# Two rwkv layers: where the convolution's products, the norm of x, adaLN and conv_in(x) stand in the order of the work

## The chip, the cores and the metric

The kernel runs on one core of one Trainium2 chip. The metric is the device time of one execution in microseconds (us), lower is better. The kernel before takes 2877.57 us (median of three runs, 2877.03 to 2883.01).

## What is computed

Two blocks of two layers each, on 256 rows of 1024 features, in float32. The change touches the first block. Each of its layers takes x and a second sequence, ctx, through the same weights (cut to what matters):

```python
mod_x = silu(c) @ ada_w[l] + ada_b[l]          # adaLN: six rows of 1024 each for x, and the same for ctx
ux = modulate(rmsnorm(x, g1), sh1, sc1) @ w_in[l]
uc = modulate(rmsnorm(ctx, g1), csh1, csc1) @ w_in[l]
prep_c = rwkv_prep(uc[..., CONV_IN:], ...)
yc, s_f, s_b = rwkv_scans(prep_c, zero, zero, emit=not last)
prep_x = rwkv_prep(ux[..., CONV_IN:], ...)
yx, _, _ = rwkv_scans(prep_x, s_f, s_b, emit=True)
mix_x = concat([conformer_conv(ux[..., :CONV_IN], ...), rwkv_out(yx, prep_x, ...)])
x = x + gt1 * (mix_x @ w_out[l])
x = x + gt2 * swiglu(modulate(rmsnorm(x, g2), sh2, sc2), wg, wu, wd)
# layer 0 only: the same for ctx, with conformer_conv(uc[..., :CONV_IN]) and rwkv_out(yc, prep_c)

def conformer_conv(u, w, b, g, h):
    val, gate = split(u, 2)
    z = dwconv(val * sigmoid(gate), w) + b     # 31 taps along the sequence, 512 channels
    return silu(group_norm(z, 8, g, h))
```

`rwkv_scans` is a recurrence over 256 positions in both directions with a 64 x 64 state for each of eight heads. `rwkv_out` is a group norm of its result, a bonus term and a gate. The second block (feed-forward, a mixer, feed-forward, with layer norms) is not touched.

## The kernel before

All weights come from device memory in pieces of 128 x 1024 floats (512 KB) through a pool of four buffers (`raw`, L356; `NRAW` is 4), issued on SyncE's queue (SP) in the order in which the pieces are used. Most of them are split by ScalarE and VectorE into a rounded part `wh` (L349) and a rest `wl` (L350), and three products replace one (`mm3`, L343). The weights of adaLN and the diagonal matrices of the convolution are used whole, straight from `raw`.

**The recurrence.** `rwkv` (L767) works in chunks of 64 positions. First come the input products (`w_in`, L642), then per pair of heads the decays and the small triangular matrices, then `inverse`, a loop of 31 steps on VectorE (two instructions each), then `reads` and `values`, and then the chain: two groups of heads, four steps each, where a state is multiplied on TensorE and updated on VectorE (L1095 to L1134). At the end (L930 and after) stand a group norm of the result (`group_norm`, L747), the bonus (L938, L939) and the gate (L940); their products take the tile `gl` and the weights `gup`.

Layer 0 runs this on ctx in the mode "wide", then on x in the mode "half". Layer 1 runs it on ctx ("all") and on x in the mode "wide". The change concerns the two wide passes: ctx of layer 0, x of layer 1. Beside a wide pass runs other work, in lane "b":

- `conv_in` (weights `wc`): the 1024 columns of the convolution's input, eight pieces, result z = value times sigmoid(gate) (L679), four tiles. In a wide pass z lies in the buffer of x0.
- `conv_pe` (weights `cd`): the 31 taps as products with diagonal matrices, 16 pieces, result in the buffer of x1, then the convolution's group norm (L753, L755, L761, L762).
- `ada_steps` (weights `ada`): 32 pieces for four of the six rows of adaLN. Four pieces make a group: 16 products of 512 columns, a copy to the tile T2b by ScalarE (L505) and eight small products of T2b, then an addition (L511).

In the kernel before these three form one row of steps, from which `fill` takes six (`FILL`) after each of the eight chain steps; what is left over comes when its results are needed. In layer 0 the norm of x (`norm_x`, its transposes are L446) is emitted at the place "post", behind the chain, and conv_in of x behind everything; the convolution of x then runs on GpSimd (POOL), tap by tap (`conv`, L732 to L737), in the background of the next half pass.

**What sets the order.** The program emits instructions; each gets a priority by its place of emission. The framework's scheduler goes through an estimated time line and gives each engine, among the instructions that it takes to be ready, the one with the foremost priority. `later(n)` moves what is emitted inside it back by n places (`LATER`, 1500). On the chip each engine, and each DMA queue, then works strictly in that order.

After the wide pass of layer 0, ctx is loaded again into x0 and x1 (L1524); after that of layer 1 the copy `keep` is (L1505). These loads stand in SP's queue among the weights and wait until z and the convolution's result have been read.

## Time and profile before

| | |
|---|---|
| median of three runs | 2877.57 us |
| the profiled execution | 2879.11 us |
| its span, first to last instruction | 2877.3 us |
| mean granted clock of TensorE | 0.959 of full speed |
| TensorE busy (products) | 2731.5 us, 95% |
| weight loads of TensorE (beside products) | 2376.7 us, 83% |
| VectorE busy | 1635.5 us, 57% |
| ScalarE busy | 1311.4 us, 46% |
| GpSimd busy | 450.9 us, 16% |
| read from device memory | 441.90 MB, 154 GB/s over the span |

Busy times are shares of the whole span, over stages with different limits; they don't say what limits a stage. For that, the timeline and the waits of the stage are read. PE is TensorE, PEld its weight loads, DVE is VectorE, ACT ScalarE, POOL GpSimd, SP SyncE. A tile's name stands without its buffer number. Products on TensorE are pipelined, so the ends given for them overlap a little.

### The profile page before, as it was taken

The numbers are of one execution on the slowest core, as the hardware profiler recorded it, in microseconds if no ns is written. First come the engines' busy times: TensorE is split into PE (matmuls) and PEld (weight loads), VectorE is DVE, ScalarE is ACT, GpSimd is POOL, SyncE is SP. The second block draws the span as 40 slices with busy tenths as digits, with TensorE's granted clock in tenths as the row PEclk, the third lists the DMA queues.
The fourth block names the chain that finished last, engine by engine and source line by source line (L and its number), as shares of the span: only waits on it lengthen the run. The fifth ranks groups of instructions, "written<-read, shape, count | busy, mean of one in ns | idle before, by whom it ended". The sixth has DMA issues, their size and how long they took to land.

```text
span 2877.3 us, 54424 instructions
## 1 busy us (share of the span) xinstructions
PE 2731.5 (95%) x22894; PEld 2376.7 (83%) x22894; DVE 1635.5 (57%) x2579; ACT 1311.4 (46%) x1990; POOL 450.9 (16%) x425
## 2 busy tenths in 40 slices
PE   7899897999989998999889999999999999999998
PEld 4886586888768897887489889889899899889897
DVE  3833367855668455842355565665655655665655
ACT  5522355443456346521244454554544544644543
POOL 0200299980121001200000000010000000100000
PEclk8989998999999999979999999999999999999999
DMA  6324642433512344213745465443465555525553
GB/s 242 113 75 144 229 171 84 170 137 133 183 67 98 128 170 169 99 60 123 251 141 189 169 206 188 166 155 110 168 200 188 179 189 185 185 81 169 198 187 120
DMA packets 123377, 447.53 MB, mean 156 GB/s; under 512 B 13686, under 2 KB 14198, under 8 KB 123132
## 3 DMA queue, kind: packets, MB, share of 16 engines
q1 hardware_dynamic: 123132, 444.06, 44.6%
q8 instruction: 179, 2.93, 0.4%
q14 instruction: 66, 0.54, 0.1%
HBM read 441.90 MB, written 2.10 MB: 154 GB/s over the span
## 4 chain that ended last, share of the span: by engine, by line
PE 83%; DVE 8%; ACT 4%; DMA 3%; issue 1%; POOL 1%; SPq 0%; ACTq 0%; DVEq 0%; POOLq 0%
PE pb L341 38%; PE acc L341 25%; PE ps L341 19%; DVE wl L350 2%; DMA raw<-in_ada 2%; DVE x L629 1%; ACT wh L349 1%; PE acc L446 0%; DVE S L965 0%; ACT L392 0%; DMA raw<-in_wr 0%; DVE S L852 0%; DVE T L963 0%; DVE T2b L628 0%; POOL tap L736 0%
## 5 line engine op out<-in xcount | busy, mean ns | idle before, releaser
L350 DVE TENSOR_TENSOR wl<-raw,wh 128x1024 fp32r<-128x1024 f32 (+1 forms) x654 | 812.0, 1245 | 629.3 <-ACT wh L349 398.3
L349 ACT CAST wh<-raw 128x1024 fp32r<-128x1024 f32 (+1 forms) x654 | 682.1, 1046 | 899.6 <-PE pb L341 344.8
L341 PE MATMUL pb<-xf,wh 128*128 128x256 f32 (+1 forms) x2560 | 485.7, 288 | 13.3 <-DVE S L639 4.0
L341 PE MATMUL pb<-S,wh 128*128 128x256 f32 x2560 | 487.5, 288 | 3.4 <-DVE S L639 1.4
L341 PEld LDWEIGHTS pb<-xf,wh 128*128 128x128 f32 (+1 forms) x2560 | 408.2, 193 | 29.1 <-DVE T1b L596 7.3
L341 PEld LDWEIGHTS pb<-S,wh 128*128 128x128 f32 x2560 | 407.8, 192 | 17.3 <-issue 8.1
L341 PE MATMUL ps<-S,wh 128*128 128x256 f32 x2048 | 391.3, 288 | 1.1 <-ACT S L468 0.9
L341 PE MATMUL pb<-xf,wl 128*128 128x256 f32 (+1 forms) x1280 | 369.5, 289 | 2.1 <-DVE wl L350 2.0
L341 PE MATMUL pb<-S,wl 128*128 128x256 f32 x1280 | 366.9, 287 | 1.6 <-DVE wl L350 1.6
L341 PEld LDWEIGHTS ps<-S,wh 128*128 128x128 f32 x2048 | 327.5, 192 | 10.8 <-issue 4.2
L341 PE MATMUL ps<-S,wl 128*128 128x256 f32 x1024 | 293.8, 287 | 1.2 <-DVE wl L350 1.2
L373 POOL TENSOR_TENSOR wl<-raw,wh 128x1024 fp32r<-128x1024 f32 x22 | 53.7, 2453 | 1367.4 <-ACT wh L372 941.1
L341 PEld LDWEIGHTS pb<-xf,wl 128*128 128x128 f32 (+1 forms) x1280 | 247.1, 193 | 8.5 <-DVE wl L350 3.5
L341 PEld LDWEIGHTS pb<-S,wl 128*128 128x128 f32 x1280 | 245.5, 192 | 5.4 <-issue 2.6
L341 PE MATMUL acc<-wh,T 128*128 128x512 f32 x704 | 206.3, 393 | 0.0
L341 PEld LDWEIGHTS ps<-S,wl 128*128 128x128 f32 x1024 | 196.8, 192 | 3.5 <-DVE wl L350 1.6
L341 PE MATMUL acc<-wh,T1b 128*128 128x512 f32 x528 | 157.6, 396 | 3.5 <-ACT T1b L349 3.5
L341 PEld LDWEIGHTS acc<-wh,T 128*128 128x128 f32 x704 | 127.0, 189 | 23.7
L736 POOL TENSOR_SCALAR tap<-z,cols 128x255 f32<-128x255 f32 (+14 forms) x120 | 143.3, 1203 | 0.0
L737 POOL TENSOR_TENSOR z<-z,tap 128x255 f32<-128x255 f32 (+14 forms) x120 | 117.6, 980 | 4.1
L341 PE MATMUL pb<-x,raw 128*128 128x254 f32 (+15 forms) x496 | 115.7, 389 | 0.0
L341 PE MATMUL acc<-wl,T 128*128 128x512 f32 x352 | 113.1, 395 | 0.0
(444 smaller groups left out, 3828.5 us busy)
## 6 DMA issues: line engine op xcount, KB each, us to landing
raw<-in_fu SPq DMA_DIRECT2D x132, 512.0 KB, 3.2
raw<-in_ada SPq DMA_DIRECT2D x96, 512.0 KB, 4.4
raw<-in_pu SPq DMA_DIRECT2D x88, 512.0 KB, 3.2
raw<-in_qu SPq DMA_DIRECT2D x88, 512.0 KB, 4.3
raw<-in_fd SPq DMA_DIRECT2D x66, 512.0 KB, 3.2
raw<-in_wr SPq DMA_DIRECT2D x51, 512.0 KB, 3.4
raw<-in_pd SPq DMA_DIRECT2D x44, 512.0 KB, 3.3
raw<-in_qd SPq DMA_DIRECT2D x44, 512.0 KB, 4.2
```

The source lines that it names most:

```text
L341: return self.nc.tensor.matmul(out, lhsT, rhs, start=start, stop=stop, **kw)
L349: self.nc.scalar.copy(hi, src)
L350: self.nc.vector.tensor_sub(lo, src, hi.bitcast(F32))
L373: self.nc.gpsimd.tensor_sub(lo, r, hi.bitcast(F32))
L629: nc.vector.tensor_add(x[b][:, s], x[b][:, s], t)
L736: nc.gpsimd.tensor_scalar(t[:, d], z[:, f, s], w(j), None, ALU.mult)
L737: nc.gpsimd.tensor_add(zc[f][:, d], zc[f][:, d], t[:, d])
```

## The change

`rwkv` gets an argument `beside`, which it calls inside `later(LATER)` right behind the rest of the input products, and so ahead of the inverse. `wide` passes a function there that emits conv_in and conv_pe of the layer whole. The chain's filler is now a row of steps given by the caller: in layer 0 the norm of x, then adaLN's 32 pieces, then conv_in of x; in layer 1 adaLN alone. What is left over is emitted when `rwkv` is done. `norm_x` at "post" and the loop over conv_in(x) behind the pass are gone, and so are the constants `QB` and `QE`.

```diff
--- before.py
+++ after.py
@@ -39,7 +39,7 @@
 
 TAPS = sorted(range(31), key=lambda j: abs(j - 15))
 
-QB, QE, QC, EVERY = (2, 3, 4, 5), (2, 3, 4, 5), (1,), 2
+QC, EVERY = (1,), 2
 
 FILL = 6
 LATER = 1500
@@ -764,7 +764,8 @@
                 put(f, ys[f])
 
 
-    def rwkv(self, l, win, s0, emit, mode, fill=lambda n=1: None):
+    def rwkv(self, l, win, s0, emit, mode, fill=lambda n=1: None, beside=lambda: None):
+
 
 
 
@@ -825,6 +826,7 @@
                 self.on("b")
             for _ in win:
                 pass
+            beside()
             self.on("r")
         AR, GR, KB = [], [], []
         Ld, Lo = slab([P, 2, 4, 4, 32]), self.S([P, 2, 4, 4, 32])
@@ -1423,26 +1425,23 @@
         fl = lambda t: t.rearrange("p (a b) -> p a b", a=4)
         z = lambda: self.t(self.pool, [P, 4, T], "z", bufs=2)
 
-        def wide(l, x, s0, ada, perm, before=None):
-
-            def filler():
-
-                steps = itertools.chain(self.conv_in(l, x, fl(self.x[0])), self.conv_pe(l, fl(self.x[0]), fl(self.x[1])),
-                                        self.ada_steps(l, ada))
-
-                def fill(n=1):
-                    lane = self.lane
-                    self.on("b")
-                    for _ in range(n):
-                        next(steps, None)
-                    self.on(lane)
-
-                return fill
+        def wide(l, x, s0, steps, perm):
+
+            def conv():
+                drain(self.conv_in(l, x, fl(self.x[0])))
+                drain(self.conv_pe(l, fl(self.x[0]), fl(self.x[1])))
+
+            def fill(n=1):
+                lane = self.lane
+                self.on("b")
+                for _ in range(n):
+                    next(steps, None)
+                self.on(lane)
 
             self.pstags = alone
-            for at in self.rwkv(l, self.w_in(l, x, RW), s0, True, "wide", filler()):
-                if at == "post" and before is not None:
-                    before()
+            drain(self.rwkv(l, self.w_in(l, x, RW), s0, True, "wide", fill, conv))
+            self.on("b")
+            drain(steps)
             self.pstags = beside
             self.on("b")
             return self.mixed_in(fl(self.x[1]), self.y, perm)
@@ -1453,22 +1452,19 @@
         cf = self.norm1(0, cf, 1, False, self.xf)
         early = []
 
-        def norm_x():
+        def then_x():
+
             zt = lambda: self.t(self.pool, [P, D], "z", bufs=2)
-            self.on("b")
             early.append(self.norm1(0, self.load("x", [zt(), zt()]), 0, False, self.Sr, keep=True))
-            self.on("r")
-
-        cm = wide(0, cf, None, QB, False, norm_x)
+            yield
+            yield from self.ada_steps(0, (2, 3, 4, 5))
+            early.append(z())
+            yield from self.conv_in(0, *early)
+
+        cm = wide(0, cf, None, then_x(), False)
         states = self.states
         self.on("b")
-        (xf,) = early
-        zx = z()
-        mods = self.ada_steps(0, [q for q in (2, 3, 4, 5) if q not in QB])
-        for _ in self.conv_in(0, xf, zx):
-            next(mods, None)
-            next(mods, None)
-        drain(mods)
+        xf, zx = early
         win = self.w_in(0, xf, RW)
         ux = next(win)
         drain(win)
@@ -1500,7 +1496,7 @@
         for b in range(2):
             nc.sync.dma_start(self.keep[b], self.x[b])
         xf = self.norm1(1, self.x, 0, True, self.xf, acc=True)
-        xm = wide(1, xf, states, QE, True)
+        xm = wide(1, xf, states, self.ada_steps(1, (2, 3, 4, 5)), True)
         for b in range(2):
             nc.sync.dma_start(self.x[b], self.keep[b])
         f = self.out(1, self.x, 0, xm)
```

Where the scheduler puts the moved work is shown at three places.

TensorE, layer 0, at the end of ctx's chain, before (`raw,csil` are adaLN's products, `const,T2b` those that close a group; `acc<-xf,S` and `ps<-S,st` belong to the chain, `S,const` to the group norm of its result):

```order
L341 MATMUL acc_458_2881<-T_456_2878,S_1786 64x64
L341 MATMUL ps_2904<-S_1098,st_2701 64x64 x2
L341 MATMUL pb_2525<-const,T2b_2523 128x2 x4
L341 MATMUL pb_2531<-raw_2532,csil 32x512 x2
L341 MATMUL ps_3008<-S_1867,const 128x256
L341 MATMUL acc_492_3014<-S_1867,const 128x256
L341 MATMUL pb_2531<-raw_2536,csil 32x512 x2
L341 MATMUL acc_459_2892<-xf_1606,S_1434 64x64
L341 MATMUL acc_459_2892<-xf_1607,S_1434 64x64
```

Now, from the last transposes of x on; the chain's last product stands 24 rows ahead of this piece:

```order
L446 MATMUL pb_2398<-const,z_2365 128x128
L446 MATMUL pb_2398<-const,z_2366 128x128
L341 MATMUL pb_2447<-raw_2448,csil 32x512 x2
L341 MATMUL pb_2447<-raw_2452,csil 32x512 x2
L341 MATMUL pb_2447<-raw_2456,csil 32x512 x2
L341 MATMUL pb_2447<-raw_2460,csil 32x512 x2
L341 MATMUL acc_532_3292<-T_531_3289,const 128x256
L341 MATMUL acc_535_3304<-T_531_3289,const 128x256
L341 MATMUL ps_3316<-T_531_3289,const 128x256
L341 MATMUL pb_2466<-const,T2b_2464 128x2 x4
L341 MATMUL acc_536_3308<-rks_1648,const 128x256
```

The first groups of adaLN stood among the chain's last products; now all of them stand behind the chain, the first products of the norm and the sixteen transposes of x, and the gate's products (`gl`, `rks`) follow the first group.

TensorE, layer 1, before:

```order
L341 MATMUL ps_14642<-S_12794,st_14439 64x64 x2
L341 MATMUL pb_14263<-const,T2b_14261 128x2 x4
L341 MATMUL pb_14269<-raw_14270,csil 32x512 x2
L341 MATMUL acc_2453_14664<-S_13563,const 128x256
L341 MATMUL acc_2455_14670<-S_13563,const 128x256
L341 MATMUL pb_14269<-raw_14274,csil 32x512 x2
L341 MATMUL acc_2448_14630<-xf_13302,S_13130 64x64
L341 MATMUL acc_2448_14630<-xf_13303,S_13130 64x64
L341 MATMUL acc_2448_14630<-xf_13302,S_13130 64x64
```

Now, from the last products of the gate on; the chain's last product stands 24 rows ahead:

```order
L341 MATMUL acc_2469_14719<-gl_11997,S_14661 128x256 x2
L341 MATMUL ps_14731<-rks_13344,const 128x256
L341 MATMUL ps_14731<-gl_11997,S_14661 128x256 x2
L341 MATMUL pb_13034<-T1b_13023,const 128x256
L341 MATMUL pb_13038<-T1b_13023,const 128x256
L341 MATMUL acc_2471_14727<-T_2461_14688,const 128x256
L341 MATMUL pb_14082<-raw_14083,csil 32x512 x2
L341 MATMUL pb_14082<-raw_14087,csil 32x512 x2
L341 MATMUL pb_14082<-raw_14091,csil 32x512 x2
L341 MATMUL pb_14082<-raw_14095,csil 32x512 x2
L341 MATMUL pb_14101<-const,T2b_14099 128x2 x4
```

Before, adaLN's groups were mixed with the chain's last step, the norm and the gate. Now the norm and the gate (`pb<-T1b,const` is the convolution's norm, `acc<-T,const` and `gl` are the recurrence's) are done when the first group begins.

SyncE's queue of transfers, layer 0, before (x_67 is x0, x_68 is x1):

```order
L356 DMA raw_2519<-in_ada 128x1024
L1524 DMA x_67<-in_ctx 128x1024
L356 DMA raw_2532<-in_ada 128x1024
L356 DMA raw_2536<-in_ada 128x1024
L356 DMA raw_2594<-in_ada 128x1024
L356 DMA raw_2598<-in_ada 128x1024
L1524 DMA x_68<-in_ctx 128x1024
L356 DMA raw_2611<-in_ada 128x1024
```

Now:

```order
L356 DMA raw_2460<-in_ada 128x1024
L1520 DMA x_67<-in_ctx 128x1024
L1520 DMA x_68<-in_ctx 128x1024
L931 DMA S_3262<-in_gup 128x1024
L356 DMA raw_2473<-in_ada 128x1024
```

Both loads of ctx and the gate's weights now stand behind the first four pieces of adaLN, ahead of the other 28.

## Rows read from the trace of the kernel before

**Rows 1.** The page: busy times, and the chain that ended last by engine.
```profile
PE 2731.5 (95%) x22894; PEld 2376.7 (83%) x22894; DVE 1635.5 (57%) x2579; ACT 1311.4 (46%) x1990; POOL 450.9 (16%) x425
...
PE 83%; DVE 8%; ACT 4%; DMA 3%; issue 1%; POOL 1%; SPq 0%; ACTq 0%; DVEq 0%; POOLq 0%
```

**Rows 2.** Windows, layer 0: us, busy PE, PEld, DVE, ACT, POOL; PEclk, DMA share, GB/s.
```profile
157.00:189.00 32.00, 32.00 (x452) 27.27 (x450) 10.37 (x18) 10.49 (x16) 1.90 (x2) 0.80 0.15 51
...
290.00:328.00 38.00, 28.70 (x140) 10.69 (x140) 6.32 (x16) 9.88 (x20) 0.00 (x0) 0.89 0.88 311
```

**Rows 3.** Timeline of SP's queue, layer 0: start, us, line, transfer, count.
```profile
275.12 0.33 SPq L1524 DMA_DIRECT2D x<-in_ctx  x1
275.54 38.32 SPq L356 DMA_DIRECT2D raw<-in_ada  x24
```

**Rows 4.** Groups of PE, 269 to 279.7 us (layer 0): busy, mean ns, idle before.
```profile
L341 PE MATMUL pb<-raw,csil 128*32 128x512 f32 x30 | 6.9, 775 | 0.2 <-DMA raw<-in_ada 0.2
...
L341 PE MATMUL pb<-const,T2b 128*128 128x2 f32 x8 | 1.1, 254 | 0.0
```

**Rows 5.** Timeline of PE, layer 0: start, us, operation, count, idle before.
```profile
269.00 3.13 PE L341 MATMUL pb<-raw,csil 128*32 128x512 f32 x16
...
279.12 0.57 PE L341 MATMUL ps<-S,xf 128*64 128x64 f32 x12
...
294.14 1.05 PE L341 MATMUL pb<-const,T2b 128*128 128x2 f32 x8 [0.74 <-ACT T2b L505]
...
321.33 1.05 PE L341 MATMUL pb<-const,T2b 128*128 128x2 f32 x8 [0.74 <-ACT T2b L505]
322.25 0.69 PE L446 MATMUL pb<-const,z 128*128 128x128 f32 x4
...
327.80 0.80 PE L341 MATMUL pb<-S,wh 128*128 128x256 f32 x2 [0.56 <-ACT T1b L462]
```

**Rows 6.** Groups of PE, 327.8 to 363 us (layer 0).
```profile
L341 PE MATMUL acc<-gl,S 128*128 128x256 f32 (+1 forms) x12 | 3.7, 411 | 0.0
L341 PE MATMUL acc<-T,const 8*128 8x256 f32 x4 | 1.4, 426 | 0.0
L341 PE MATMUL ps<-gl,S 128*128 128x256 f32 (+1 forms) x4 | 1.3, 428 | 0.0
```

**Rows 7.** Timeline of POOL, layer 0.
```profile
343.35 0.94 POOL L732 TENSOR_SCALAR z<-z,cols 128x256 f32<-128x256 f32 x1 [5.75 <-DVE z L679]
...
346.59 0.73 POOL L939 TENSOR_TENSOR S<-S,T 128x256 f32<-128x256 f32 x1
347.26 0.30 POOL L890 MEMSET rks<- 128x256 f32 x1
```

**Rows 8.** Windows, 460 to 470 us, columns as in the second group.
```profile
460.00:470.00 10.00, 3.69 (x63) 3.11 (x66) 10.00 (x13) 3.66 (x8) 10.00 (x9) 0.80 0.00 0
```

**Rows 9.** Waits of PE, 430 to 485 us: total, times, longest.
```profile
PE ps L341 <- DVE S L851: 10.1, 3, 5.5
```

**Rows 10.** Windows, layer 1, columns as in the second group.
```profile
1255.00:1290.00 35.00, 33.95 (x426) 28.99 (x426) 10.38 (x23) 11.52 (x19) 0.95 (x1) 0.57 0.10 31
```

**Rows 11.** Groups of PE, 1357.7 to 1372.62 us (layer 1).
```profile
L341 PE MATMUL pb<-raw,csil 128*32 128x512 f32 x30 | 8.7, 905 | 1.2 <-DMA raw<-in_ada 1.2
```

**Rows 12.** Groups of PE, 1372.6 to 1394.4 us (layer 1).
```profile
L341 PE MATMUL pb<-raw,csil 128*32 128x512 f32 x36 | 8.5, 647 | 0.0
L341 PE MATMUL pb<-const,T2b 128*128 128x2 f32 x16 | 2.1, 254 | 0.8 <-ACT T2b L505 0.8
```

**Rows 13.** Timeline of PE, layer 1.
```profile
1372.06 0.56 PE L341 MATMUL ps<-S,xf 128*64 128x64 f32 x10
...
1398.77 1.05 PE L341 MATMUL pb<-const,T2b 128*128 128x2 f32 x8 [0.74 <-ACT T2b L505]
...
1420.70 1.05 PE L341 MATMUL pb<-const,T2b 128*128 128x2 f32 x8 [0.74 <-ACT T2b L505]
```

## Prediction

> **What bounds the kernel now.** I read the page first: TensorE is busy 95% of the span and carries 83% of the chain that ended last [rows 1]. So the kernel is a row of tensor products, and what a reordering can win or lose are the places where TensorE waits or does another stage's work late. A measurement of this kernel can tell about 0.2%, that is 5.75 us, from no change; the three runs lie within 6 us.
>
> Then I took windows over the two stretches that the change touches. In layer 0 the inverse and what follows it fill TensorE: from 157 to 189 us it is busy throughout [rows 2]. Then follow the chain steps, whose last state product ends at 279.12 + 0.57 = 279.69 us [rows 5], and the adaLN stretch. There, from 290 to 328 us, TensorE is busy 28.70 of 38 us, and the DMA share is 0.88 at 311 GB/s [rows 2]: this stretch waits for weights of 512 KB each, 32 in all, in eight groups of four. From the fourth group's closing product at 294.14 to the eighth's at 321.33 us [rows 5] four groups take 27.19 us, so 6.8 us each. The first group is covered, since four buffers hold its weights early: its sixteen products took 3.13 us, from 269.00 us on [rows 5], in the middle of the chain's tail. SP's queue issues the last 24 loads from 275.54 us on, over 38.32 us [rows 3].
>
> Layer 1 looks the same: the chain's last product ends at 1372.06 + 0.56 = 1372.62 us, the last adaLN group closes at 1420.70 + 1.05 = 1421.75 us, and three groups between 1398.77 and 1420.70 us take 7.3 us each [rows 13].
>
> **The part that costs nothing: the convolution in front of the inverse.** The diff suggests that the products of conv_in now fill the inverse. The order of instructions says that they did so before: before and after, the eight weights of ctx's conv_in stand among the inverse's rows, and TensorE is full there [rows 2], so nothing is won. What moves is the end of the diagonal products: before they ended early in the chain, now they are handed out one by one over all its steps. The products are the same. I price it at zero, covered by the chain's waits for VectorE; if they stood bare, the chain would be longer by their delay, and what came behind them as filler, adaLN, is the next thing late. That is the cost I work out now.
>
> **Layer 1, adaLN after the norms.** In the kernel before, part of adaLN lies in the tail of the chain: 8.7 us of products and 1.2 us of waiting for weights [rows 11], and with one group's closing products, 1.1 us as in layer 0 [rows 4], 11.0 us by 1372.62 us. In the new order none is left there, so the chain ends at about 1372.6 - 11.0 = 1361.6 us. Behind it stand first, without adaLN between, the rest of the convolution's norm and the whole norm and gate of the chain's output. Before, that stretch lasted 21.8 us with 8.5 + 2.1 + 0.8 = 11.4 us of adaLN in it [rows 12]. So it takes at least 10.4 us, if TensorE is its limit, and at most 21.8 us, if the steps of VectorE and ScalarE (square, root, reciprocal, scale) are. I take 14 us, nearer the lower end, because adaLN's products in that stretch also held up the norm's, which stand behind them in one row on TensorE, and add nothing for the convolution's norm, whose steps run beside it. AdaLN then starts at 1375.6 us. Its first group takes 3.13 + 1.05 = 4.2 us [rows 5], the seven others 7 x 6.8 = 47.6 us by layer 0's pace; the last ends at 1427.4 us instead of 1421.75: **5.7 us later**. With the norms at 10.4 us it is 2.1 us, with 21.8 us 13.5 us, and with layer 1's own pace of 7.3 us 3.5 us more. TensorE goes on at once with the output projection, so this delay is paid in full.
>
> **Layer 0, adaLN with the norm of x ahead and conv_in(x) behind.** The part of adaLN in the chain's tail is 6.9 + 0.2 + 1.1 = 8.2 us [rows 4], so the chain ends at 279.7 - 8.2 = 271.5 us. Ahead of adaLN now stand products of the norm (about 3 us, an estimate from four that took 1.4 us [rows 6]) and the sixteen transposes of x, which before took from 322.25 to 327.80 us, 5.55 us with their evacuation [rows 5]. Start 280.0, end 280.0 + 4.2 + 47.6 = 331.8 us; before, conv_in(x) started at 327.80 [rows 5]. So its start is about 4 us later. But the gate's products and the norm's that stood in it, 3.7 + 1.4 + 1.3 = 6.4 us [rows 6], are now in adaLN's shade, where TensorE has idle time. Conv_in(x) ends 4.1 - 6.4 = **2.3 us earlier**. Bounds: +4.1 us if nothing of the 6.4 is saved, -6.4 us if the start is not late.
>
> Two queues are passed here. SP: both loads of ctx back into x0 and x1, and the gate's weights, now stand ahead of the last 28 adaLN loads, where before only x1's stood ahead of the last 24, issued at 275.12 us [rows 3]. The load into x1 waits for the convolution's norm, whose last products now stand two rows behind the chain's last; that is 271.5 us plus a few, still ahead of the start of adaLN, so I cost it at zero. If it came later, each us would delay seven groups by one. POOL: it begins the convolution of x at 343.35 us, as soon as the first tile of conv_in(x) is there, and then works on it without a pause; the four additions and two fills that stood among its first taps [rows 7] move ahead: two times 0.73 and two times 0.30 us, 2.1 us less. That matters, since at 460 to 470 us POOL is busy all the time and TensorE only 3.69 of 10 us [rows 8], waiting 10.1 us for the keys' tile that POOL's backlog delays [rows 9]. The first tile comes 4.1 us later for the start and, as I estimate, 5 of the 6.4 us sooner for the foreign products, so POOL is about 3 us early, and lets the 2.3 us through.
>
> Everything else moves by single rows; zero.
>
> **Sum.** +5.7 - 2.3 = +3.4 us on the profiled execution's 2879.11 us, 2882.5 us. That execution is 1.54 us above the median of the runs, 2877.57 us; against the median the forecast is **2881.0 us**, 0.12% more.
>
> **Rival: slower, by the norms of layer 1 laid bare.** Both norms now run in a row before adaLN, and TensorE is a strict row of products: if each root and reciprocal is waited for, the stretch of 14 us becomes 21.8 us, and layer 1 pays 13.5 us, in sum +11.2 us, **2888.8 us**. It decides from 16.4 us on (14 + 5.75 - 3.4). For it: before, this stretch did last 21.8 us, and the last scaling waited for VectorE. Against it: half of that was adaLN's own products. The Trainium skill, "Perfetto Trace Analysis", section Optimization Strategy, says that stretches with different limiting engines gain from being interleaved; the change separates a stretch bound by transfers from one bound by the engines' latency. By that rule alone layer 0 would lose too; the 6.4 us that it takes into adaLN's shade speak against it there.
>
> **Rival: faster, by the clock and the filled waits.** From 1255 to 1290 us TensorE was busy 33.95 of 35 us at a granted clock of 0.57 [rows 10], so mostly at 1.2 GHz, and from 157 to 189 us at 0.80 [rows 2]. If the diagonal products, handed out evenly, keep the clock at 2.4 GHz, up to 35 x 0.43 = 15 us and 32 x 0.20 = 6.4 us are to be had. With half of that, 10.7 us, the sum is 3.4 - 10.7 = -7.3 us, **2870.3 us**. For it: the diagonal products are wide, the chain's are narrow. Against it: the stretch at 0.57 lies before most of them in either order. The Trainium skill, "TensorE: Matmul & The Clock Gate", section What's actually happening, says that the clock is throttled unless activity releases it; the busy but slow stretch shows that a busy row alone does not tell.
>
> **Rival: nothing.** The scheduler has put the convolution in front already; what adaLN loses in the chain's tail it gets back because the chain ends earlier by it, and the sum is within 2 us of zero: 2877.6 us.
>
> **How the numbers follow.** Forecast 0.50, slower rival 0.20, faster rival 0.20, nothing 0.10. The forecast's own bounds run from 2.1 - 6.4 = -4.3 to 13.5 + 4.1 = +17.6 us, most of it between -2 and +9 us: of its 0.50 I put 0.38 within 5.75 us, 0.11 above, 0.01 below. The faster rival gives 0.18 to faster and 0.02 to the same, the slower one 0.20, nothing 0.10. So faster 0.19, same 0.50, slower 0.31. The likeliest case's own range is 2875.5 to 2886.5 us. For 8 in 10 the range reaches into both rivals: 2868 to 2891 us.
>
> **What would show it.** In the new profile the chain of layer 1 should end near 1361 us plus the shift of layer 0, adaLN's first product come some 14 us behind it, its groups follow at 6.8 to 7.3 us, and the output projection start 3 to 8 us later relative to the chain's start. In layer 0 adaLN should start near 280 us, conv_in(x) near 332 us, and run without foreign products. A conv_in(x) that starts after 338 us, a stretch of over 17 us between chain and adaLN in layer 1, or a chain with a clock well above 0.57 at its start would each prove a step wrong.

## The result: 1.5% slower, outside the range

The changed kernel takes 2920.35 us (median of four runs, 2916.09 to 2923.1), the kernel before on the same chip 2877.3 us (median of four, 2869.38 to 2883.01). The ratio is 1.015, interval 1.0123 to 1.0178: **43 us slower**. The forecast was 2881.0 us, the slower rival 2888.8, the top of the range 2891.

The page of the changed kernel first: busy times, and the chain that ended last.

```profile
span 2921.3 us, 54434 instructions
...
PE 2758.5 (94%) x22894; PEld 2387.2 (82%) x22894; DVE 1640.9 (56%) x2579; ACT 1310.7 (45%) x1990; POOL 449.3 (15%) x425
...
PE 79%; DVE 7%; ACT 5%; POOL 4%; DMA 3%; issue 2%; SPq 0%; ACTq 0%; DVEq 0%; POOLq 0%
```

TensorE has the same number of products and is busy 27 us longer (2731.5 before); so the larger part of the 43 us is products that take longer, the rest idle time. Where it arises is read from SP's queue, which issues the same weights in the same order behind the changed stretch; the table holds the first issue of a stage's weights in the two traces.

| SP issues | before | after | later by |
|---|---|---|---|
| first piece of conv_in(x), `wc` | 316.31 | 351.84 | 35.5 |
| first of the half pass's input weights, `wr` | 345.89 | 370.16 | 24.3 |
| a middle piece of the feed-forward behind the half pass, `fu` | 573.66 | 607.80 | 34.1 |
| layer 1's ctx pass, `wr` | 1102.15 | 1137.02 | 34.9 |
| layer 1's output projection and feed-forward, `fu` | 1432.09 | 1476.44 | 44.4 |

So in these two executions **24 us arise in the wide pass of layer 0, 10 more in the half pass behind it, and 10 in the wide pass of layer 1**. Layer 1's share is the least certain: in `thenx_only` below, where the program emits layer 1 as the kernel before does, the same stretch is 11 us longer (340.90 against 329.94 us).

What TensorE does in layer 0 is read from the window from 100 us to the first issue of `wr`, first before, then changed (columns as in [rows 2]):

```profile
100.00:345.89 245.89, 230.26 (x2550) 175.60 (x2549) 101.93 (x229) 80.29 (x146) 9.87 (x16) 0.91 0.42 146
100.00:370.16 270.16, 251.69 (x2523) 179.45 (x2516) 103.11 (x232) 82.02 (x148) 10.18 (x16) 0.86 0.38 131
```

TensorE is idle for 15.6 us of the first window and for 18.5 us of the second. So only 2.8 of the 24 us are idle time; 21.4 us are products that take longer (2550 and 2523 of them), and the mean granted clock is 0.86 instead of 0.91. In the half pass it is the other way round: TensorE is busy 718.8 and 718.9 us, and the growth is idle time.

Layer 0. The first fence is TensorE's timeline of the changed kernel, with each row's start and length, and in brackets the wait before it; it answers to [rows 5].

```profile
279.81 0.57 PE L341 MATMUL ps<-S,xf 128*64 128x64 f32 x13
...
287.19 1.09 PE L446 MATMUL pb<-const,z 128*128 128x128 f32 x8 [0.45 <-ACT T1b L462]
289.56 1.92 PE L341 MATMUL pb<-raw,csil 128*32 128x512 f32 x16 [1.28 <-issue]
...
293.13 1.05 PE L341 MATMUL pb<-const,T2b 128*128 128x2 f32 x8
294.05 1.19 PE L341 MATMUL acc<-rks,const 128*128 128x256 f32 x2
295.03 2.21 PE L341 MATMUL ps<-gl,S 128*128 128x256 f32 x4
297.17 2.37 PE L341 MATMUL acc<-gl,S 128*128 128x256 f32 x4
...
303.64 2.21 PE L341 MATMUL ps<-gl,S 128*128 128x256 f32 x4
305.78 3.63 PE L341 MATMUL pb<-raw,csil 128*32 128x512 f32 x12
...
313.09 1.87 PE L341 MATMUL pb<-const,T2b 128*128 128x2 f32 x8 [0.69 <-ACT T2b L505]
...
319.11 1.05 PE L341 MATMUL pb<-const,T2b 128*128 128x2 f32 x8 [0.80 <-ACT T2b L505]
...
356.35 1.05 PE L341 MATMUL pb<-const,T2b 128*128 128x2 f32 x8 [0.74 <-ACT T2b L505]
357.30 0.50 PE L341 MATMUL pb<-S,wh 128*128 128x256 f32 x2
```

The chain ends at 280.38 us, not at 271.5. AdaLN begins at 289.56 us, not at 280.0. Its first group's closing products start at 293.13 and its second's at 313.09: 20 us, where 6.8 were priced. Between them stand the gate's products, 11.7 us from 294.05 to 305.78. Conv_in(x) starts at 357.30 instead of about 332. The next fence holds windows of the changed kernel, the one behind it two of the kernel before (columns as in [rows 2]).

```profile
157.00:189.00 32.00, 31.01 (x444) 27.05 (x442) 11.89 (x23) 10.94 (x17) 1.90 (x2) 0.72 0.15 51
...
269.00:290.00 21.00, 18.50 (x223) 12.04 (x223) 15.09 (x36) 14.13 (x29) 0.00 (x0) 1.00 0.15 52
290.00:328.00 38.00, 34.71 (x119) 13.70 (x111) 10.61 (x25) 8.17 (x19) 5.13 (x8) 0.60 0.58 198
```

```profile
247.00:269.00 22.00, 21.32 (x321) 14.68 (x319) 11.20 (x25) 8.91 (x16) 0.00 (x0) 0.90 0.14 50
269.00:290.00 21.00, 20.16 (x158) 9.95 (x156) 9.35 (x23) 7.25 (x15) 0.00 (x0) 0.94 0.84 302
```

From 269 to 290 us the weights flowed at 302 GB/s before and at 52 now. Such a lull is not new: before, it lay from 247 to 269 us, at 50 GB/s, and SP's queue waited in it 23.2 us at once for TensorE to free a buffer. It now lies 20 us later. What is lost is what followed it: before, the loads started again while TensorE still had the rest of the chain and the norm to do; now the chain and most of the norm are done when they start again. From 290 to 328 us the granted clock is 0.60 (0.89 before, [rows 2]): mostly 1.2 GHz, in a stretch in which TensorE is busy longer than before. SP's queue of the changed kernel says why nothing was loaded:

```profile
244.94 19.27 SPq L356 DMA_DIRECT2D raw<-in_ada  x4
264.27 21.40 SPq L1520 DMA_DIRECT2D x<-in_ctx  x2
285.71 0.43 SPq L931 DMA_DIRECT2D S<-in_gup  x1
290.65 1.75 SPq L356 DMA_DIRECT2D raw<-in_ada  x4
```

Four pieces of adaLN fill the four buffers by 264 us. The queue then stands at the loads of ctx, 21.0 us of it in one wait for VectorE's work on the convolution's norm (L753); and without that wait the buffers would not have come free either, since the products that read them stand behind the chain and the norms.

Layer 1, TensorE's timeline of the changed kernel (34.9 us are layer 0's delay):

```profile
1380.28 4.37 PE L341 MATMUL pb<-x,raw 128*128 128x245 f32 x20
...
1385.53 0.64 PE L341 MATMUL ps<-S,xf 128*64 128x64 f32 x16
...
1401.00 2.21 PE L341 MATMUL acc<-gl,S 128*128 128x256 f32 x4
...
1412.01 3.64 PE L341 MATMUL pb<-raw,csil 128*32 128x512 f32 x16
```

The chain ends at 1386.17, less 34.9 that is 1351.3, where 1361.6 was forecast and 1372.62 stood before [rows 13]. Both norms and the gate then last 25.8 us until adaLN begins (14 forecast, 21.8 as the bound), and the last group closes at 1464.68, so adaLN lasts 52.7 us (51.8 forecast).

### The profile page after: what moved, and what is told of

It reads as the page before. It is cut to its first block, busy times and chain, and to the rows that moved or that the text cites. A ratio compares the mean times of both kernels' runs of the same rounds, so it can differ in the third digit from the quotient of the medians.

```text
span 2921.3 us, 54434 instructions
## 1 busy us (share of the span) xinstructions
PE 2758.5 (94%) x22894; PEld 2387.2 (82%) x22894; DVE 1640.9 (56%) x2579; ACT 1310.7 (45%) x1990; POOL 449.3 (15%) x425
## 4 chain that ended last, share of the span: by engine, by line
PE 79%; DVE 7%; ACT 5%; POOL 4%; DMA 3%; issue 2%; SPq 0%; ACTq 0%; DVEq 0%; POOLq 0%
PE pb L341 35%; PE acc L341 25%; PE ps L341 19%; DMA raw<-in_ada 2%; POOL tap L736 2%; DVE wl L350 2%; POOL z L737 1%; DVE x L629 1%; ACT wh L349 1%; ACT L392 0%; PE acc L446 0%; DVE S L854 0%; DVE T L965 0%; DVE S L967 0%; DMA raw<-in_wr 0%
## 5 line engine op out<-in xcount | busy, mean ns | idle before, releaser
L736 POOL TENSOR_SCALAR tap<-z,cols 128x255 f32<-128x255 f32 (+14 forms) x120 | 152.2, 1277 | 0.0
L341 PE MATMUL pb<-x,raw 128*128 128x254 f32 (+15 forms) x496 | 124.7, 394 | 0.0
L341 PEld LDWEIGHTS acc<-wh,T1b 128*128 128x128 f32 x528 | 95.2, 190 | 22.4 <-ACT T1b L349 4.4
```

Of the source, the lines that this page charges most:

```text
L341: return self.nc.tensor.matmul(out, lhsT, rhs, start=start, stop=stop, **kw)
L736: nc.gpsimd.tensor_scalar(t[:, d], z[:, f, s], w(j), None, ALU.mult)
```

## The experiments

Theory A: the 43 us come from **where the diagonal products end**. Emitted ahead, but at a priority 1500 back, they keep the weight buffers in their order of emission and are handed out to the end of the chain, so the products of all 32 pieces of adaLN come behind it, bare. Theory B: they come from **the new filler** (norm of x, adaLN, conv_in(x) in one row), with its loads past SP's queue. Theory C, for the half pass: GpSimd's convolution of x starts later and holds the rest up. Diffs are against the changed kernel unless another is named.

### One part at a time

Only layer 1 changed (`l1_only`); only the convolution ahead, norm of x at "post" and conv_in(x) behind the pass as before (`conv_only`); only the new filler, with the convolution's steps at its head as before (`thenx_only`). All three use one switch (cut to it):

```diff
-        def wide(l, x, s0, steps, perm):
+        def wide(l, x, s0, steps, perm, ahead=True, post=None):
...
+            if not ahead:
+                steps = itertools.chain(self.conv_in(l, x, fl(self.x[0])),
+                                        self.conv_pe(l, fl(self.x[0]), fl(self.x[1])), steps)
...
-            drain(self.rwkv(l, self.w_in(l, x, RW), s0, True, "wide", fill, conv))
+            for at in self.rwkv(l, self.w_in(l, x, RW), s0, True, "wide", fill, conv if ahead else lambda: None):
+                if at == "post" and post is not None:
+                    post()
```

> The change in layer 1 alone (x's pass); layer 0 as in the kernel before. Theory A (the diagonal products, now of lower priority but emitted ahead, keep adaLN's weight buffers until the chain is over, so that adaLN starts bare): layer 1 cost 10 us in the changed kernel, from a shift of 35 us ahead of it to one of 45 us behind it; this kernel should be 8 to 12 us slower than before, about 2888. Rival B (the norm of x and the gate ahead of adaLN in layer 0 are the cost, and layer 1 suffers only from layer 0's disturbance, e.g. its clock): within 4 us of before.

> The convolution's products emitted in front of the inverse in both layers, but the norm of x back at its place behind the chain and conv_in(x) back behind the pass, so the filler is adaLN alone. Theory A: the move of the convolution carries the loss; 25 to 45 us slower than before, 2903 to 2922. Rival B (norm of x, gate and conv_in(x) in the filler are what costs in layer 0): only layer 1's 10 us, at most 15 us slower, below 2893.

> The reverse: the convolution's products stay the first steps of the chain's filler as before, and behind them stand the norm of x, adaLN and conv_in(x). Theory A: the diagonal products end early as before; within 10 us of before, 2868 to 2888. Rival B: 15 to 35 us slower than before, 2893 to 2912.

| kernel | median | kernel before beside it | ratio, interval |
|---|---|---|---|
| l1_only | 2883.96 | 2879.68 | 1.0023 (1.0006 to 1.0041) |
| conv_only | 2910.72 | 2879.68 | 1.0115 (1.0094 to 1.0136) |
| thenx_only | 2893.63 | 2879.68 | 1.0049 (1.0030 to 1.0067) |

The convolution ahead makes 31 us without the new filler, the filler 14 us without the convolution ahead; 45 together, close to the 43 of both. `conv_only` lies in A's range. `thenx_only` is 4 us above A's range and at the lower edge of B's, and `l1_only`, 4.3 us, lies between B's and A's, next to B's. `conv_only` brings layer 0's adaLN to the place that layer 1's has: from its timeline,

```profile
259.05 3.96 PE L341 MATMUL pb<-x,raw 128*128 128x245 f32 x18
...
284.94 3.64 PE L341 MATMUL pb<-raw,csil 128*32 128x512 f32 x16
```

the last long row of diagonal products at 259.05 (before, adaLN's first products stood at 269.00, [rows 5]), then the norms, then adaLN bare from 284.94 us on; the gate's products stand behind adaLN here, from 354.77 us on. Its window from 290 to 328 us shows a clock of 0.59 with 30.10 of 38 us busy, and of the 21.0 us that layer 0 is late at `wr`, 10.8 are idle time. That is A's picture, and most of the loss. B's part is smaller, and not where B looks for it: `thenx_only` issues layer 0's `wr` 2.6 us earlier than the kernel before, and its half pass is 14 us longer (770.53 against 756.26 us).

### The convolution's priority

`late1000` and `late1200` are the changed kernel whole, but what is emitted ahead gets a priority 1000 or 1200 back instead of 1500:

```diff
-            beside()
             self.on("r")
+        with self.later(1000):
+            self.on("b" if wide else self.lane)
+            beside()
+            self.on("r")
```

> The changed kernel, but the convolution's products go back by 1000 places of priority instead of 1500, so that their last diagonal product stands ahead of half of the chain in both layers (as in the kernel before) and adaLN's first product inside the chain. Everything else of the change is kept. Theory A: most of the 43 us comes back, 2870 to 2890. Rival B: it stays 20 us or more slower than before, above 2897. Rival C (the diagonal products handed out one by one between the chain's narrow products make those slower, wherever they end): no more than half of the loss comes back, 2895 to 2915.

> The changed kernel with the convolution's products moved back by 1200 places of priority: the last diagonal product stands early in the chain again (as with 1000 places), but adaLN's first product just behind the chain's last state products instead of ahead of them. Theory A (the buffers are what holds adaLN): near the kernel with 1000 places, within 10 us of before. Theory A2 (it is not the buffers but that adaLN stands behind the chain, bare, for whatever reason): 10 to 25 us slower than before.

`late1000`: 2876.74 us, ratio 0.9997 (0.9978 to 1.0015): all 43 us are back. `late1200`: 2891.84 us, 1.0045 (1.0026 to 1.0063), 13 us. `late1000` lies in A's range. In the traces adaLN of layer 0 begins 14.5 us ahead of the chain's end with 1000, 3.1 us ahead of it with 1200 and 9.2 us behind it with 1500. The timeline and two windows of `late1000`:

```profile
269.44 1.93 PE L341 MATMUL pb<-raw,csil 128*32 128x512 f32 x16
272.63 1.05 PE L341 MATMUL pb<-const,T2b 128*128 128x2 f32 x8
...
283.28 0.64 PE L341 MATMUL ps<-S,xf 128*64 128x64 f32 x16
283.85 1.05 PE L341 MATMUL pb<-const,T2b 128*128 128x2 f32 x8
...
297.43 0.70 PE L341 MATMUL acc<-rks,const 128*128 128x256 f32 x2
...
301.33 1.22 PE L341 MATMUL ps<-gl,S 128*128 128x256 f32 x4
302.48 1.05 PE L341 MATMUL pb<-const,T2b 128*128 128x2 f32 x8
...
327.55 1.05 PE L341 MATMUL pb<-const,T2b 128*128 128x2 f32 x8 [0.74 <-ACT T2b L505]
328.50 0.50 PE L341 MATMUL pb<-S,wh 128*128 128x256 f32 x2
```

```profile
247.00:269.00 22.00, 21.63 (x332) 15.88 (x331) 12.93 (x29) 12.98 (x27) 0.69 (x1) 0.92 0.01 2
290.00:328.00 38.00, 31.31 (x158) 12.31 (x154) 8.58 (x22) 9.46 (x17) 3.51 (x6) 0.96 0.79 284
```

AdaLN begins at 269.44 us, one group closes ahead of the chain's last product and the second right at it, and conv_in(x) starts at 328.50, against 327.80 before. The lull is there as well, 2 GB/s from 247 to 269 us, and costs nothing here. The new filler is all in this kernel, and the total is level, but the filler is not free: in the profiled execution `wr` comes 4.5 us earlier than before, the half pass is 10 us longer (766.38 us), and the wide pass of layer 1 is 11 us shorter. Read over the kernels, TensorE's last diagonal product of layer 0 and adaLN's first product stand so:

| kernel | last diagonal product ends | adaLN starts | chain's last product ends |
|---|---|---|---|
| before | 246.90 | 269.00 | 279.69 |
| late1000 | 241.74 | 269.44 | 283.92 |
| late1200 | 247.23 | 274.52 | 277.57 |
| thenx_only | 245.05 | 273.61 | 276.03 |
| conv_only | 265.44 | 284.94 | 259.12 |
| changed | 263.85 | 289.56 | 280.38 |

AdaLN starts 20 to 29 us behind the last diagonal product in every one of them, whatever stands between. In the first four kernels adaLN so begins ahead of the chain's end, in the last two behind it. What the runs show is the place: **with the convolution's products 1500 places back, where they end 17 us later and adaLN begins behind the chain, the kernel loses most of the 43 us; with 1000 places and everything else kept, it loses nothing**.

What in that place costs is less sure. `late1200` was to tell the buffers (A) from adaLN's place behind the chain (A2). Its diagonal products end where those of the kernel before do (247.23 and 246.90 us) and it is 13 us slower, which is in A2's range and not in A's. Nor does that prove A2, since adaLN still begins 3.1 us ahead of the chain's end, layer 0's `wr` is only 1.9 us late, and the rest arises behind it. And in `l1_only` layer 1's adaLN begins 26 us behind the chain (1368.17 against 1342.50 us), but the chain ends so much earlier that the whole costs 4.3 us. That the four buffers are the means (a fifth set for adaLN alone) was not tried.

A rival stays open: the clock. From 100 us to `wr` the mean granted clock is 0.91 before, 0.92 in `late1000`, 0.93 in `thenx_only` and 0.90 in `late1200`, but 0.85 in `conv_only` and 0.86 in the changed kernel. So of these, the two orders that lose most in layer 0 have the lowest clock. No run holds the order and changes the clock, so how much of the loss is the lost overlap and how much the slower products isn't shown.

### AdaLN in turn with the convolution

If transfers are what adaLN lacks, its pieces could stand between the diagonal products. `zip1000` and `zip1200` do so with 1000 and 1200 places, and take adaLN out of the chain's filler (cut to the heart of it):

```diff
-                drain(self.conv_pe(l, fl(self.x[0]), fl(self.x[1])))
+                cd, ada = self.conv_pe(l, fl(self.x[0]), fl(self.x[1])), self.ada_steps(l, (2, 3, 4, 5))
+                for _ in cd:
+                    next(ada, None)
+                drain(ada)
```

> As the kernel with 1000 places, but in both layers adaLN's steps are emitted in turn with the diagonal products (one piece of the diagonals, two of adaLN), so that the weights of adaLN are loaded while the diagonal products keep TensorE busy; the filler of the chain holds only the norm of x and conv_in(x) in layer 0, nothing in layer 1. If adaLN's bare transfers are what costs (theory A): the 9 us idle in layer 0 and 7 us in layer 1 of the adaLN stretch go, and its slow clock with them; 10 to 30 us faster than before, 2850 to 2868. If TensorE's own work is the limit throughout: within 6 us of before.

> The same with 1200 places: the chain's steps come earlier against the diagonal and adaLN products. Theory A: like the one with 1000 places within 10 us, 10 to 30 us faster than before. Rival C (diagonal products handed out among the chain's narrow ones cost): slower than the kernel with 1000 places by 5 us or more, since more of them stand among chain products.

Both missed: 2903.8 us, 1.0083 (1.0063 to 1.0103), and 2892.27 us, 1.0044 (1.0026 to 1.0062). `zip1000` has a granted clock of 0.95 from 100 us to `wr`, above the 0.91 of the kernel before, and is still slower, so the clock alone does not order the kernels. The Trainium skill, "Perfetto Trace Analysis", section Optimization Strategy, says that stretches bound by different engines may gain from being interleaved; here the interleaved orders are 25 and 14 us slower than the kernel before, and the one that only lets adaLN overlap the chain's tail is level with it. In `zip1200` layer 0 is 5.7 us early at `wr`; the half pass then loses 8 us and layer 1 another 11, where the copies of `keep` into x0 and x1 are issued at 1401 us and later. That these copies are the cause was not tested. Why `zip1000` loses was not followed further.

### The gate's products between two groups of adaLN

`gateforce` keeps the changed order, but in layer 0 issues the gate's products behind the last closing product of adaLN (kept in `closing`); `after_gate` does so in both layers.

```diff
-                self.mm(pb[:, 0, :], self.cst("hindT")[:, f * P : f * P + P], rks)
-                self.mm(pb[:, 1, :], gup[:, f * P : f * P + P], gl[:, 0, :], True, False)
+                with self.tc.issue_after(self.closing.ins) if wide and l == 0 else contextlib.nullcontext():
+                    self.mm(pb[:, 0, :], self.cst("hindT")[:, f * P : f * P + P], rks)
+                    self.mm(pb[:, 1, :], gup[:, f * P : f * P + P], gl[:, 0, :], True, False)
```

> The changed kernel, with one constraint added in layer 0: the gate's products of ctx are issued only behind the last closing product of adaLN, so that they no longer stand between adaLN's first and second group. In the changed kernel the second group closed 20 us behind the first, where a later one takes 7. If the gate's products hold up adaLN's loads (four buffers, one row on TensorE): adaLN ends about 12 us earlier, conv_in(x) has some 6 us of foreign products again, and the kernel is 4 to 12 us faster than the changed one, 2908 to 2916. If the second group waits for its weights whatever stands in between: within 3 us of the changed kernel.

> The changed kernel with the gate's products issued behind adaLN's last closing product in both layers, not in layer 0 alone. Theory G (the gate's products ahead of adaLN's groups keep adaLN's weights from being loaded in layer 1 too): 4 to 12 us faster than the kernel with that constraint in layer 0 alone (2906), so 2894 to 2902. Rival H (in layer 1 the gate only changes places, since the output projection needs it at once): within 4 us of 2906.

`gateforce`: 2906.3 us, 14 us less than the changed kernel (1.0102 against before, 1.0071 to 1.0134); `after_gate`: 2905.37 us, 1.011 (1.0087 to 1.0134). So taking the gate out from between two groups gains some 14 us in layer 0, 2 us more than forecast, and in layer 1 nothing that can be told. The size is rough, since the intervals of `gateforce` and of the changed kernel overlap. The timeline and the window of `gateforce`:

```profile
286.89 1.92 PE L341 MATMUL pb<-raw,csil 128*32 128x512 f32 x16 [0.66 <-ACT T1b L462]
...
291.50 1.05 PE L341 MATMUL pb<-const,T2b 128*128 128x2 f32 x8
...
297.82 1.05 PE L341 MATMUL pb<-const,T2b 128*128 128x2 f32 x8 [0.69 <-ACT T2b L505]
...
336.88 1.05 PE L341 MATMUL pb<-const,T2b 128*128 128x2 f32 x8 [0.74 <-ACT T2b L505]
338.31 1.22 PE L341 MATMUL ps<-gl,S 128*128 128x256 f32 x4
```

```profile
290.00:328.00 38.00, 31.61 (x146) 10.26 (x148) 3.85 (x14) 4.33 (x8) 1.25 (x1) 0.91 0.94 334
```

Seven groups now take 45.4 us, 6.5 each, at 334 GB/s and a clock of 0.91. The gate's four products take 1.22 us instead of 2.21. But adaLN still starts at 286.89 us. Two things changed at once, the block's place and the clock, and this run does not part them. `late1000` gives a hint: there most of the gate's products also stand in one block, from 297.43 to 302.55 us, at full clock, and the two groups around it take 7.8 us each. By the forecast's pace of 6.8 us for a group's weights, I estimate that a block of 5 us fits beside one group's loads and one of 11.7 us doesn't.

Would the same help the good orders? `late1000_gate` and `before_gate` put the gate behind adaLN in both layers of `late1000` and of the kernel before.

> The kernel with 1000 places, with the gate's products issued behind adaLN in both layers. Theory G, if the gate's products cost wherever they stand among adaLN's groups: 3 to 10 us faster than without the constraint, 2866 to 2873. Rival H (they cost only where adaLN starts behind the chain, on a clock at half speed): within 3 us of 2877.

> The kernel before with the same constraint in both layers. Theory G: 3 to 10 us faster than before, 2867 to 2874. Rival H: within 3 us of before.

No: 2899.62 us, 1.0078 (1.0060 to 1.0097), 23 us above `late1000`; and 2886.05 us, 1.0035 (1.0018 to 1.0053), 12 us above the kernel before. Theory G missed by the sign, H by the size. In layer 0 of the kernel before the gate stood behind adaLN already [rows 6], so there the constraint acts in layer 1. In `late1000` most of the gate's products stood ahead of a group's closing products, where they cost little; moved, they stand among conv_in(x) and the output projection. That TensorE has no wait to give there is argued and not shown. In `late1000_gate` the `wr` weights come 8.9 us later than in `late1000` (350.24 against 341.39), and the mean clock up to there is 0.86 instead of 0.92, so here too the clock stands as a rival.

### The better order in layer 1 alone

`mix1000` and `mix800` leave layer 0 as it was and put the convolution ahead in layer 1, at 1000 or 800 back (the two edits shown above, joined).

> Layer 0 as in the kernel before; layer 1 with the convolution's products emitted in front of the inverse but moved back by 1000 places instead of 1500. In the kernel that did so in both layers, layer 1 gained 13 us (from 6 us late to 7 us early). If layer 1's gain is its own: 8 to 15 us faster than before, 2862 to 2871. If it came from what layer 0 left behind: within 5 us of before.

> The same with 800 places: in the order all diagonal products and the convolution's norm then stand ahead of the first chain step. If an earlier end of the diagonal products only helps (theory A): as fast as the one with 1000 places or faster, 2855 to 2871. If the chain's waits then lack filler: slower than that by 5 us or more, 2870 to 2890.

2875.03 us, 0.9996 (0.9977 to 1.0014), and 2874.25 us, 0.9996 (0.9982 to 1.0010), twelve executions each: no change, as the rival said; `mix800` is as fast as `mix1000` and so has no loss for want of filler either. The gain that I expected came from one profiled execution of `late1000`, whose layer 1 was 11 to 13 us shorter, depending on where it is read. The profiled execution of `mix1000` has a shorter layer 1 as well, by 5 us (324.67 against 329.94 us), and took 2866.45 us, but its median shows no gain. No order that I ran is measurably faster than the kernel before.

### GpSimd's queue in the half pass

`few_before` and `few_after` leave out 15 of the 30 side taps of GpSimd's convolution.

```diff
-            for i, j in enumerate(TAPS[1:]):
+            for i, j in enumerate(TAPS[1:16]):
```

> The kernel before with 15 instead of 30 side taps in the convolution of x that GpSimd does in layer 0 (the other taps are left out, so half of GpSimd's work there is missing). Between 440 and 480 us TensorE was busy only 24.5 of 40 us, waiting behind GpSimd's queue. If that queue sets the end there: 8 to 20 us faster than before. If the waits only change their name: within 4 us.

> The changed kernel with the same 15 taps left out. The distance to the kernel before with so many taps left out tells what GpSimd's queue adds: in the changed kernel the delay of layer 0 grew from 24 us at the end of conv_in(x) to 35 us in the half pass. If GpSimd's queue makes that growth: 30 to 36 us between the two. If it is the order of VectorE's and TensorE's instructions in the half pass: 40 to 46 us as before.

`few_before` was to be 8 to 20 us faster if GpSimd set the end; it took 2884.51 us, 1.0024 (1.0011 to 1.0037). GpSimd's busy time fell from 450.9 to 321.0 us and nothing was won: TensorE's waits for the keys' tile are 12.6 us in `few_before`. So GpSimd's length does not bound the half pass of the kernel before. `few_after` took 2912.8 us, 28.3 us more than `few_before`, in place of 43, which misses both ranges. Between the two the delay is 23.8 us at the half pass's `wr` and 25.2 us at layer 1's: it grows by 1.4 us, where with all taps it grows by 10.6. That looks as if the growth needed GpSimd's long queue, but the lengths speak against it. The half pass of the changed kernel takes 766.9 us with all taps and 767.0 with half of them; it is the kernel before whose half pass got longer without the taps, from 756.3 to 765.5 us, at a clock of 0.95 instead of 0.97. So these two runs do not show what makes the growth. It isn't the late start carried on: `thenx_only` and `late1000` reach `wr` 2.6 and 4.5 us **earlier** than the kernel before and layer 1 11.7 and 5.6 us later. The wait that grows in the changed kernel, from its table of waits (us, times, longest; [rows 9] before), is

```profile
PE ps L341 <- DVE S L853: 15.1, 4, 6.8
```

and it is one of several. With half the taps it is as long (15.3 us in `few_after`). What holds it is open.

## Why the prediction was wrong

- **Bound of the kernel, "this stretch waits for weights":** right in part. Of TensorE's 9.3 us of waits from 290 to 328 us before, 3.8 us end with weights and 3.7 us with ScalarE's copy to T2b. I read that TensorE waits there, and did not ask what runs beside the loads: from 269 to 290 us, where they flowed at 302 GB/s beside the chain's tail, they now flow at 52, and no chain is left when they start again.
- **"I price it at zero, covered by the chain's waits for VectorE"** failed, and it is the step that carried most. With the diagonal products handed out over the whole chain, adaLN comes behind it, and `conv_only`, which moves only the convolution, loses 31 us; `late1000`, which has them end earlier, loses nothing. Of the 24 us of layer 0, 21.4 are longer products and 2.8 idle time; the price of the slower clock among them is not shown apart. I did work out "adaLN is the next thing late", but with a chain that ends 8.2 us earlier to pay for it.
- **Layer 0, "the chain ends at 279.7 - 8.2 = 271.5 us"** and with it **"Start 280.0"** failed: 280.38 and 289.56 us. The 8.2 us of adaLN did leave, and other products grew in their place. These groups are TensorE's from 100 us to the end of the chain, first of the kernel before, then of the changed one:

```profile
L341 PE MATMUL pb<-x,raw 128*128 128x255 f32 (+15 forms) x248 | 59.3, 394 | 0.0
...
L341 PE MATMUL ps<-S,xf 128*64 128x64 f32 x128 | 6.7, 231 | 0.0
...
L341 PE MATMUL acc<-st,S 64*64 64x64 f32 x96 | 5.1, 225 | 0.0
```

```profile
L341 PE MATMUL pb<-x,raw 128*128 128x255 f32 (+15 forms) x248 | 65.0, 396 | 0.0
...
L341 PE MATMUL ps<-S,xf 128*64 128x64 f32 x128 | 8.1, 227 | 0.0
...
L341 PE MATMUL acc<-st,S 64*64 64x64 f32 x96 | 6.8, 228 | 0.0
```

  The diagonal products are busy 5.7 us longer, these two groups of the chain 3.1, with the same length of a single product (394 and 396 ns). They overlap less, since wide and narrow ones now alternate one by one near the chain's end; that is argued from the rows, no run changed it alone. It isn't what decides: in `conv_only` the chain ends at 259.12, earlier than forecast, and 31 us are lost. But the longer products are part of the 24 us.
- **"are now in adaLN's shade, where TensorE has idle time"** failed. A shade needs the engine to reach those products while it waits; here they stand between the first and the second group as one block, at half clock, 11.7 us, and adaLN's next loads wait for the buffers that only the products behind the block free. Priced at -6.4 us, the order with the block costs 14 (`gateforce`), with the clock's part in it not told apart.
- **SP, "If it came later, each us would delay seven groups by one":** the condition came true (the queue stood for 21.0 us at ctx's loads), but the products stood later still, so it was not the bound by itself.
- **POOL "lets the 2.3 us through"** failed: the half pass added 10 us, and 10 to 14 us in kernels that reach it early (`late1000`, `thenx_only`). I had taken one wait, 10.1 us [rows 9], for the whole of that stage, and GpSimd's queue for its cause, which halving the taps does not bear out.
- **Layer 1:** the net was about right by two errors. The chain ended 10 us earlier than forecast, its last 6 us at a clock of 1.00, and the norms took 25.8 us, 4 us over the upper bound; adaLN's length was off by 0.9 us. Forecast +5.7, bounds 2.1 to 13.5; `l1_only` +4.3, the changed kernel +10. The bound of 21.8 us came from a stretch in which adaLN's products kept TensorE at work; bare, the gate's products ran at 2.21 us for four there as well.
- **Slower rival**, by norms of layer 1: its mechanism occurred (25.8 us), its price, +13.5 us, was mostly paid back by the early end of the chain. The loss it missed is the same one in layer 0, where I let the gate speak against it. **Faster rival**, by the clock: no gain; from 157 to 189 us the clock is 0.72 instead of 0.80 [rows 2], and the clock of 1.00 up to 290 us is followed by 0.60. The range held neither the size nor the stage of the loss, because it took layer 0's step as a matter of -6.4 to +4.1 us.

## What to carry to other kernels

When filler is emitted earlier but at a lower priority, look at where it **ends**, and what then comes behind it: here adaLN, which waits in part for transfers, lost the chain's tail that had run beside its loads. A lull in the transfers alone is no sign of it: 50 GB/s before, 2 in `late1000` and 52 in the changed kernel, in windows of 21 and 22 us. Look at what TensorE has left to do when the loads start again. Foreign products are in the shade of a waiting stage only as far as they fit beside its loads: 5 us in one block cost little in `late1000`, 11.7 us at half clock cost more in the changed kernel. And split a stage's loss into idle and busy time before naming its cause: here most of layer 0's was busy time, at a lower clock. One execution with a layer 1 shorter by more than 10 us was no gain in the median of twelve, so a profile's good stage is to be timed before it is built upon.

## What was not expected of the hardware

- The granted clock was 0.60 from 290 to 328 us with 34.71 of 38 us busy, and 0.91 in `gateforce`, also in adaLN, with 31.61 us busy. The busier stretch had the lower clock. The Trainium skill, "TensorE: Matmul & The Clock Gate", section What's actually happening, ties the release of the throttle to activity; these two rows show that the busy share of a window alone does not tell it. Four of the gate's products took 2.21 us in the one and 1.22 us in the other, so slower products themselves make a window busier.
- Executions of one kernel spread by some 8 us to either side (29 of the kernel before: 2868.84 to 2884.34), so totals are compared here by medians, and a stage's shift of ten us in one execution is weak evidence by itself.
